# A hybrid attention block on one core: order of logits, norm pieces, sums and feed-forward products

## The chip, the cores and the metric

One core of one Trainium2 chip. The metric is device time in microseconds (us), the median of several executions. The engines are TensorE (PE, matmul; PEld is its weight load), VectorE (DVE), ScalarE (ACT), GpSimd (POOL) and SyncE (SP), which issues most DMAs here.

## What is computed

One layer over 16 learned meta tokens and 1024 frames (L = 1040, D = 1024, 8 heads of 64, feed-forward width FF = 2816), all in float32. Cut to what matters:

```python
n1 = _rmsnorm(h, norm1_w)
q, k, v, fg, u = jnp.split(n1 @ w_in, [D_ATTN, 2 * D_ATTN, 3 * D_ATTN, 3 * D_ATTN + N_HEADS], axis=-1)
# q and k are RMS-normed per head; cum_logf = cumsum(log_sigmoid(fg + b_fgate))
s = q @ k.T * scale + (cum_logf[t] - cum_logf[s])        # causal, per head
a_out = softmax(s) @ v
p_out = pooled(u) @ w_pool * pool_scale                  # trailing means minus self
h = h + jnp.concatenate([a_out, p_out], axis=-1) @ w_out
n2 = _rmsnorm(h, norm2_w)
h = h + (silu(n2 @ w_gate) * (n2 @ w_up)) @ w_down       # the meta tokens are dropped
```

## The kernel before, in words

Everything is kept transposed (features on partitions, tokens on the free axis). A float32 operand is split into a high part and a rest (fp32r), and a product is three products on TensorE: high by high, rest by high, high by rest. No scheduler reorders anything: the order in which the Python code issues instructions is the order on each engine's queue, and the tables at the top of the file (`MAXN`, `FILL`, `XN`, `XW`, `PRE`, ...) set it.

**Ramp.** Norm 1, then the projections. `v_mm` (L248) makes v for 128 tokens, 24 products of 512 columns. Behind the third block of v stand the sums of squares over the features, for the norm: 18 products of 2 columns (L281, L282; the result of a token lies on its partition) and six of a third of the tokens (L294, L295; the result lies in a row), each row evacuated by VectorE to `qrow` (L296).

**Attention.** The work is cut in 16 *units*, (head, half): units 0 to 7 are the eight heads for the first 512 query tokens, with 640 keys, units 8 to 15 the same heads for the second 512, with 1040 keys. A unit has three things:

- `stack` (L581): six loads of Q and K from DRAM and two small ones, issued by SyncE into new slots.
- `mx_steps` (L613): the logits by query rows, in chunks, for the rows' maximum: products `s`, each followed by a maximum on VectorE into `mp`. Then `mt` (L640) transposes the maximum (`Mc`) into the rows of Q that the next thing uses. In units 0 to 7 these are 5 chunks, in units 8 to 15 9 chunks.
- `sp_steps` (L658): the logits by key rows, in steps: `st` products, two exponentials on ScalarE (`ph`, `p32`), their rest `pl` on GpSimd or VectorE, and some steps later the value products `pv`, with the last of a unit followed by the division. A unit of the first half has 3 steps, one of the second half 7.

The head loop (L1188 on) goes through the units' steps. While unit n's steps run, `max_next(MAXN[n][x])` issues so many chunks of the maxima of the units ahead; `fill` issues `FILL[n]` of a product job per step of the output projection (`o` products, with loads `wos` of its weights and `h` of the residual); `work` takes one piece from a list of background pieces for SwiGLU's norm (sums of squares, `n2`, scaling, splitting of h); `vload` (L597), at step 2, issues the load of v for unit n+1 into one of two alternating slots, `vhb[h % 2]`, which the value products of unit n-1 have to have left. At the top of a unit `stack` is issued for unit n+3 (n < 6) or n+2. SyncE carries out its queue in order, so a load that waits holds up what stands behind it.

**SwiGLU.** The gate and up products of a pair of feature blocks and their weights, over both token halves, are done by a scheme with seven products for eight (`SEQ7`; `w_prep`, L1077, makes the sums and differences of the weights on VectorE and splits them; `t_pieces`, L1173, makes those of the tokens, T1 to T4). The first pair is done by all eight ordinary products (`first_pair`, L1246), first for token half 0, then, when half 1 is normed, for half 1. Between the two, `run_stream(0, 4 * PRE)` does those products of the next `PRE` pairs that need token half 0 alone (j = 1, 2). The norm of half 1 hangs on `t` (L850), which VectorE makes from the sum of squares. Then the down projection follows.

Of the kernel before, what the change touches and what calls it, by code (L numbers as in the profile page):

```python
# [8 lines left out]
FR = mybir.dt.float32r  # L9
AF = mybir.ActivationFunctionType  # L10
OP = mybir.AluOpType
AX = mybir.AxisListType

D = 1024
KT = D // 128
# [8 lines left out]
ST = 9  # L24
# [1 line left out]
BIG = 1e30  # L26
CH3 = ((0, 348), (348, 346), (694, 346))
CHQ = ((16, 512), (528, 512))
PRE = 1
VC, VK = 640, 6  # L30
SQ = 4
RA, LW = 10, 4
# [2 lines left out]
TL = 3  # L35
HL, LL, LS = 8, 5, 2
LA = 3
MAXN = [(2, 2, 1)] * 7 + [(3, 3, 3)] + [(2, 2, 1, 1, 1, 1, 1)] * 8
SUBV = 4
MID = 1  # L40
VST = 3
AGE = 2
RAMP = 1
FILL = [8 / 24] * 8 + [12 / 35] * 5 + [4 / 14] * 2 + [2 / 7]
CJ, XW, XN = {1: (0, 1), 2: (2, 3), 3: (4, 5), 4: (6, 7)}, 2, 12


@with_exitstack
def block_kernel(ctx, tc, hT, n1w, w_f, w_v, w_u, w_qk, b_f, qnw, knw, w_pool, pscale, w_out, n2w, w_g, w_up, w_d, outT):
# [12 lines left out]
    def ut(cols, dt=FT, s="u"):  # L62
        return U.tile([128, cols], dt, tag="u", bufs=NU, padded_shape=None, name=nm(s))
# [4 lines left out]
    def ps(s="ps"):  # L68
        return PSP.tile([128, 512], FT, tag="ps", name=nm(s))
# [175 lines left out]
    vst, vsd = [], DR.tile([ST, 128, 192 * NH], FT, name="vsd")  # L245
    rcol = const([128, ST], FT, "rcol")

    def v_mm(j):  # L248
        sz = min(128, L - 128 * j)
        T = slice(128 * j, 128 * j + sz)  # L250
        p = ps("v")
        for k in range(KT):
            vh, vl = wv[k // 2]
            W = slice(512 * (k % 2), 512 * (k % 2) + 512)
            mm(p[:sz], xh[k][:, T], vh[:, W], start=k == 0, stop=False)  # L255
            mm(p[:sz], xh[k][:, T], vl[:, W], start=False, stop=False)
            mm(p[:sz], xl[k][:, T], vh[:, W], start=False, stop=k == KT - 1)
        return p

    def v_evac(j, p):  # L260
# [8 lines left out]
            V.scalar_tensor_tensor(t[:sz, :, 128:192], src, rcol[:sz, j:j + 1], f(t)[:sz, :, 0:64], op0=OP.mult, op1=OP.subtract)  # L269
            nc.sync.dma_start(vsd[j, :sz, 768 * i:768 * i + 768], f(t)[:sz].rearrange("p h c -> p (h c)"))  # L270

    v0, v1, vp = v_mm(0), v_mm(1), v_mm(2)


    acch, accl = split_w(sqacc, L, ut, A, V)
    rb = ut(L, FT, "rb")
    qrow = ut(L, FT, "qrow")
    pc = ps()
    for j in range(ST):
        sz = min(128, L - 128 * j)  # L280
        mm(pc[:sz, 2 * j:2 * j + 2], acch[:, 128 * j:128 * j + sz], ones[:, 0:2], start=True, stop=False)  # L281
        mm(pc[:sz, 2 * j:2 * j + 2], accl[:, 128 * j:128 * j + sz], ones[:, 0:2], start=False, stop=True)  # L282
    qcol = const([128, ST], FT, "qcol")
    rtmp = const([128, ST], FT, "rtmp")
    V.memset(qcol, 1.0)
# [3 lines left out]
    A.activation(rcol, qcol, AF.Ln)  # L289
    A.activation(rcol, rcol, AF.Exp, scale=-0.5)  # L290
    rsqrt_newton(rcol, qcol, rtmp)
    for c, (o, n) in enumerate(CH3):
        p = ps()
        mm(p[:, :n], ones, acch[:, o:o + n], start=True, stop=False)  # L294
        mm(p[:, :n], ones, accl[:, o:o + n], start=False, stop=True)  # L295
        V.tensor_scalar(qrow[:, o:o + n], p[:, :n], 1.0 / D, EPS, op0=OP.mult, op1=OP.add)  # L296

    qkd = {c: DR.tile([NP, 2, 128, L], FT, name=f"{c}d") for c in "qk"}  # L300
# [280 lines left out]
    def stack(h, b):  # L581


        dma = nc.sync.dma_start
        T, B = slice(0, 64), slice(64, 128)
        R = (T, B)[h % 2]
        n = 640 + 400 * b
        Q, K1, K2 = ut(1024, FR, "Q"), ut(n, FR, "K1"), ut(n, FR, "K2")
        Q1, Q2 = Q[:, :512], Q[:, 512:]
        heads[h, b] = Q1, Q2, K1, K2  # L590
        q, k = [[qkd[c][h // 2, a, R, S] for a in range(2)] for c, S in (("q", slice(512 * b, 512 * b + 512)), ("k", slice(0, n)))]
        for t, P, src in ((Q1, T, q[0]), (K1, T, k[0]), (Q1, B, q[0]), (K1, B, k[1]), (Q2, T, q[1]), (K2, T, k[0])):
            dma(f(t)[P], src)
        dma(f(Q2)[64:66], f(KAT[0])[4 * h + 2:4 * h + 4, :512])
        dma(f(K2)[64:68], f(KAT[0])[4 * h:4 * h + 4, :n])

    def vload(h, b):  # L597
        for t, j, n, sz in ((0, 0, 5, 128), (1, 5, 3, 128), (1, 8, 1, 16))[:1 + 2 * b]:
            o, nj = j - 5 * t, 5 - t
            if vhb[h % 2][t] is None:  # L600
                vhb[h % 2][t] = ut(192 * nj, FR, "vh").rearrange("p (j c) -> p j c", c=192)
            nc.sync.dma_start(f(vhb[h % 2][t])[:sz, o:o + n], vsd[j:j + n, :sz, 192 * h:192 * h + 192].rearrange("j p c -> p j c"))

    bg = []
# [191 lines left out]
    for k in range(KT):  # L796
        W = slice(128 * k, 128 * k + 128)
        for p, (o, n) in zip(pb, CHQ):
            mm(p[:, :n], wcur[0][:, W], xh[k][:, o:o + n], start=k == 0, stop=False)
            mm(p[:, :n], wcur[1][:, W], xh[k][:, o:o + n], start=False, stop=False)  # L800
            mm(p[:, :n], wcur[0][:, W], xl[k][:, o:o + n], start=False, stop=k == KT - 1)
        turn()
        if k == 0:
            psplit[0] = split_w(pooled[0], SEQ, ut, A, V)
            h_load(0)
            wo[1] = out_load(1)
        if k == 1:
            h_load(1)
            stack(*units[0])
            vload(*units[0])  # L810
            stack(*units[1])
        if 2 <= k < 6:
            pool_map(5 - k)
        if k == 6:
            wo[0] = out_split(wo[0])
# [67 lines left out]
    def work(n):  # L883

        while n and (pq or dl):
            now, dl[:] = dl[:], []
            if pq:
                pq.pop(0)[1]()
            for _, g in now:
                g()  # L890
            n -= 1
# [41 lines left out]
    def finish(age):  # L933
        while fins and fins[0][2] <= step - age:
            u, g, _ = fins.pop(0)
            g()
            ready.add(u)
# [257 lines left out]
    for n, (h, b) in enumerate(units):  # L1195
        while (h, b) not in ready:
            if any(u == (h, b) for u, _, _ in fins):
                finish(0)
            else:
                max_next(1)  # L1200
        while len(heads) < min(len(units), n + (4 if n < 6 else 3)):
            stack(*units[len(heads)])
        if n == len(units) - 1:
            pq.extend((None, lambda u=u, c=c: w0_prep(u, c)) for c in (11, 21, 12, 22) for u in range(2))
            w0_load()
        for x, (front, mid, back, end) in enumerate(sp_steps(h, b)):
            step += 1
            finish(AGE)
            front()
            now, ends[:] = ends[:], []  # L1210
            mids.append(mid)
            if len(mids) > MID:
                mids.pop(0)(V if step % SUBV == 0 or n == len(units) - 1 else G)
            if n == len(units) - 1 and x:
                work(XW)
            elif n >= XN:
                work(1)
            flush()
            max_next(MAXN[n][x])
            for e in now:  # L1220
                e()
            behind.append((back, end))
            if len(behind) > LA:
                g, e = behind.pop(0)
                g()
                if e:
                    e[0]()
                    ends.append(e[1])
            background(3)
            if x == 2 and n + 1 < len(units):  # L1230
                vload(*units[n + 1])
            share += FILL[n]
            while share >= 1:
                fill(1)
                share -= 1
# [64 lines left out]
        if k >= W1:  # L1300
            w_ahead(k - KT)
    first_pair(0, second_half)
    run_stream(0, 4 * PRE)
    first_pair(1, lambda k: None)
    w0.clear()
    stores()
    run_stream(4 * PRE, len(stream))
    stores()


# [145 lines left out]
```

## Time and profile before

| | us |
|---|---|
| median of 3 executions | 1162.12 |
| the three | 1162.23, 1158.40, 1162.12 |
| the profiled execution | 1158.39 |
| its span in the profile | 1156.6 |
| mean granted clock of TensorE | 0.987 |
| TensorE busy (5327 matmuls) | 1123.7 (97%) |
| VectorE, ScalarE, GpSimd busy | 788.0 (68%), 486.1 (42%), 228.0 (20%) |
| chain that ended last: TensorE, VectorE, ScalarE, DMA | 89%, 4%, 3%, 1% |

The profile is of one execution. Its busy times tell how much of the span an engine worked; the waits tell what ended an engine's idle time; the stretches tell both for a part of the span. The granted clock is 1.00 at TensorE's full speed of 2.4 GHz and 0.50 at 1.2 GHz.

### The profile page before, as it was taken

How to read it: one execution, taken by the hardware profiler on the slowest of the kernel's cores; microseconds unless marked ns; L12 is line 12 of the kernel's file. 1: busy time of each engine (PE TensorE's matmuls, PEld its weight loads, DVE VectorE, ACT ScalarE, POOL GpSimd, SP SyncE). 2: the span in 40 equal slices, each digit the busy share in tenths (PEclk: the TensorE clock that was granted, in tenths of full speed). 3: DMA queues.
4: the chain of work that ended last, by engine and by line, in shares of the span. 5: the costliest groups of instructions: out<-in, count | busy, mean ns of one | idle time of the engine just before them, and what ended most of it. 6: DMA issues, size and time to landing. Idle time of an engine off the chain costs nothing.

```text
span 1156.6 us, 14780 instructions
## 1 busy us (share of the span) xinstructions
PE 1123.7 (97%) x5327; PEld 932.7 (81%) x5327; DVE 788.0 (68%) x1292; ACT 486.1 (42%) x883; POOL 228.0 (20%) x189
## 2 busy tenths in 40 slices
PE   7999999999999988898999999999999999999998
PEld 6778899788878876686888888888888888888886
DVE  7655874776655659747976666656665669778986
ACT  7344531535545655635433232223223335343541
POOL 0011244134336744220011001201120110000000
PEclk9999999999989998998999999999999999999999
DMA  7133340677655473050213132312231379543452
GB/s 239 75 143 134 128 151 24 180 219 186 165 145 149 111 215 115 28 164 19 100 56 109 55 100 64 110 55 92 73 100 64 113 272 370 189 157 101 153 193 110
DMA packets 72825, 151.15 MB, mean 131 GB/s; under 512 B 8752, under 2 KB 24752, under 8 KB 72752
## 3 DMA queue, kind: packets, MB, share of 16 engines
q1 hardware_dynamic: 62928, 133.91, 37.0%
q10 hardware_dynamic: 9824, 16.30, 3.9%
q8 instruction: 42, 0.69, 0.2%
q14 instruction: 31, 0.25, 0.1%
HBM read 115.13 MB, written 34.77 MB: 130 GB/s over the span
## 4 chain that ended last, share of the span: by engine, by line
PE 89%; DVE 4%; ACT 3%; DMA 1%; issue 1%; SPq 0%; POOL 0%; ACTq 0%; DVEq 0%; POOLq 0%
PE gu L1103 11%; PE gu L1104 11%; PE gu L1102 11%; PE d L1363 6%; PE d L1365 6%; PE d L1364 6%; PE pj L448 3%; PE pj L449 3%; PE pj L447 3%; PE o L502 2%; PE o L501 2%; PE o L503 2%; PE s L632 2%; PE st L684 1%; PE s L629 1%; PE v L255 1%
## 5 line engine op out<-in xcount | busy, mean ns | idle before, releaser
L1103 PE MATMUL gu<-cb,ws 128*128 128x512 f32 x560 | 220.8, 394 | 0.0
L1104 PE MATMUL gu<-cb,ws 128*128 128x512 f32 x560 | 220.7, 394 | 0.0
L1102 PE MATMUL gu<-cb,ws 128*128 128x512 f32 x560 | 220.4, 394 | 0.0
L1092 ACT ACTIVATE ws<-wst 128x512 fp32r<-128x512 f32 x120 | 70.2, 622 | 142.1 <-DVE wst L1087 96.3
L1093 DVE TENSOR_TENSOR ws<-wst,ws 128x512 fp32r<-128x512 f32 x120 | 82.5, 688 | 63.6 <-ACT ws L1092 63.6
L1103 PEld LDWEIGHTS gu<-cb,ws 128*128 128x128 f32 x560 | 105.3, 188 | 24.9 <-DVE ws L1093 0.4
L1102 PEld LDWEIGHTS gu<-cb,ws 128*128 128x128 f32 x560 | 105.3, 188 | 24.4
L1104 PEld LDWEIGHTS gu<-cb,ws 128*128 128x128 f32 x560 | 105.3, 188 | 24.1
L1363 PE MATMUL d<-hd,wd 128*128 128x512 f32 x308 | 121.1, 393 | 0.0
L1365 PE MATMUL d<-hd,wd 128*128 128x512 f32 x308 | 120.9, 393 | 0.0
L1364 PE MATMUL d<-hd,wd 128*128 128x512 f32 x308 | 120.8, 392 | 0.0
L1116 POOL TENSOR_TENSOR e<-e,e 128x512 f32<-128x512 f32 x20 | 29.1, 1457 | 333.4 <-DVE e L1129 174.1
L633 DVE TENSOR_REDUCE mp<-s 128x1 f32<-128x264 f32 (+8 forms) x112 | 54.0, 505 | 40.8 <-PE s L632 38.8
L698 POOL TENSOR_TENSOR pl<-p,ph 128x512 fp32r<-128x512 f32 (+4 forms) x58 | 69.9, 1213 | 48.0 <-ACT p L692 33.8
L448 PE MATMUL pj<-xh,wl 128*128 128x346 f32 (+2 forms) x216 | 72.9, 337 | 0.0
L449 PE MATMUL pj<-xl,wh 128*128 128x346 f32 (+2 forms) x216 | 72.9, 337 | 0.0
L447 PE MATMUL pj<-xh,wh 128*128 128x346 f32 (+2 forms) x216 | 72.9, 337 | 0.0
L691 ACT ACTIVATE ph<-st 128x512 fp32r<-128x512 f32 (+3 forms) x88 | 46.2, 525 | 54.5 <-PE st L684 52.5
L1365 PEld LDWEIGHTS d<-hd,wd 128*128 128x128 f32 x308 | 57.8, 188 | 13.2
L1364 PEld LDWEIGHTS d<-hd,wd 128*128 128x128 f32 x308 | 57.9, 188 | 13.1
L1363 PEld LDWEIGHTS d<-hd,wd 128*128 128x128 f32 x308 | 57.8, 188 | 12.9
L1032 ACT ACTIVATE hd<-wst 128x512 fp32r<-128x512 f32 x77 | 48.0, 623 | 36.0 <-issue 26.8
(279 smaller groups left out, 2421.8 us busy)
## 6 DMA issues: line engine op xcount, KB each, us to landing
wst<-in_w_d SPq DMA_DIRECT2D x77, 256.0 KB
wst<-in_w_g SPq DMA_DIRECT2D x22, 512.0 KB
wst<-in_w_up SPq DMA_DIRECT2D x22, 512.0 KB
wst<-hidd SPq DMA_DIRECT2D x22, 512.0 KB
vh<-vsd SPq DMA_DIRECT2D x16, 480.0 KB
K<-kd SPq DMA_DIRECT2D x24, 260.0 KB
vsd<-vst SPq DMA_DIRECT2D x16, 384.0 KB
Q<-qd SPq DMA_DIRECT2D x48, 128.0 KB
```

Of the source, the lines that this page charges most:

```text
L447: mm(p[:, :n], wh[:, W], xh[k][:, o:o + n], start=k == 0, stop=False)
L448: mm(p[:, :n], wl[:, W], xh[k][:, o:o + n], start=False, stop=False)
L449: mm(p[:, :n], wh[:, W], xl[k][:, o:o + n], start=False, stop=k == KT - 1)
L698: sub.tensor_tensor(pl[:sz, o0:o1], p32[:sz, o0:o1], f(ph)[:sz, o0:o1], op=OP.subtract)
L1092: A.activation(t[:, :512], src, AF.Copy)
L1093: E.tensor_tensor(t[:, 512:], src, f(t)[:, :512], op=OP.subtract)
L1102: mm(p, w[:, W], c[:, :512], start=k == 0, stop=False)
L1103: mm(p, w[:, Wl], c[:, :512], start=False, stop=False)
L1104: mm(p, w[:, W], c[:, 512:], start=False, stop=k == 3)
L1363: mm(p, w[:, W], h[:, LO], start=i == 0, stop=False)
L1364: mm(p, w[:, Wl], h[:, LO], start=False, stop=False)
L1365: mm(p, w[:, W], h[:, HI], start=False, stop=i == NPR - 1)
```

## The change

Five things are edited. `MAXN`: in the first half 2 chunks at each of the three steps of a unit, for 2, 2 and 1 (and 3, 3, 3 at unit 7). `XN`, `XW`: from unit 10 on (for unit 12) one background piece is taken at the head of each step, ahead of the `st` products, for one behind them, and the last unit takes no longer two; `FILL` spreads the output projection's jobs otherwise. `PRE`: the j = 1, 2 products of pairs 1 and 2 (for pair 1) come first in the stream, and 4 of the 8 still stand ahead of `first_pair(1)`, the other 4 behind it and ahead of the products with T's. The sums in the ramp stand one behind each product of the third block of v, with `qrow` ahead of `qcol` on VectorE. The four slots of v are allocated in the ramp, for at the first loads.

```diff
--- before.py
+++ after.py
@@ -26,7 +26,7 @@
 BIG = 1e30
 CH3 = ((0, 348), (348, 346), (694, 346))
 CHQ = ((16, 512), (528, 512))
-PRE = 1
+PRE = 2
 VC, VK = 640, 6
 SQ = 4
 RA, LW = 10, 4
@@ -35,14 +35,14 @@
 TL = 3
 HL, LL, LS = 8, 5, 2
 LA = 3
-MAXN = [(2, 2, 1)] * 7 + [(3, 3, 3)] + [(2, 2, 1, 1, 1, 1, 1)] * 8
+MAXN = [(2, 2, 2)] * 8 + [(2, 2, 1, 1, 1, 1, 1)] * 8
 SUBV = 4
 MID = 1
 VST = 3
 AGE = 2
 RAMP = 1
-FILL = [8 / 24] * 8 + [12 / 35] * 5 + [4 / 14] * 2 + [2 / 7]
-CJ, XW, XN = {1: (0, 1), 2: (2, 3), 3: (4, 5), 4: (6, 7)}, 2, 12
+FILL = [9 / 24] * 8 + [9 / 21] * 3 + [8 / 35] * 5
+CJ, XW, XN = {1: (0, 1), 2: (2, 3), 3: (4, 5), 4: (6, 7)}, 2, 10
 
 
 @with_exitstack
@@ -245,16 +245,18 @@
     vst, vsd = [], DR.tile([ST, 128, 192 * NH], FT, name="vsd")
     rcol = const([128, ST], FT, "rcol")
 
-    def v_mm(j):
+    def v_mm(j, between=()):
+        between = list(between)
         sz = min(128, L - 128 * j)
         T = slice(128 * j, 128 * j + sz)
         p = ps("v")
         for k in range(KT):
             vh, vl = wv[k // 2]
             W = slice(512 * (k % 2), 512 * (k % 2) + 512)
-            mm(p[:sz], xh[k][:, T], vh[:, W], start=k == 0, stop=False)
-            mm(p[:sz], xh[k][:, T], vl[:, W], start=False, stop=False)
-            mm(p[:sz], xl[k][:, T], vh[:, W], start=False, stop=k == KT - 1)
+            for a, (x, w) in enumerate(((xh, vh), (xh, vl), (xl, vh))):
+                mm(p[:sz], x[k][:, T], w[:, W], start=k + a == 0, stop=k + a == KT + 1)
+                if between:
+                    between.pop(0)()
         return p
 
     def v_evac(j, p):
@@ -269,17 +271,28 @@
             V.scalar_tensor_tensor(t[:sz, :, 128:192], src, rcol[:sz, j:j + 1], f(t)[:sz, :, 0:64], op0=OP.mult, op1=OP.subtract)
             nc.sync.dma_start(vsd[j, :sz, 768 * i:768 * i + 768], f(t)[:sz].rearrange("p h c -> p (h c)"))
 
-    v0, v1, vp = v_mm(0), v_mm(1), v_mm(2)
+    v0, v1 = v_mm(0), v_mm(1)
 
 
     acch, accl = split_w(sqacc, L, ut, A, V)
     rb = ut(L, FT, "rb")
     qrow = ut(L, FT, "qrow")
     pc = ps()
-    for j in range(ST):
+
+    def col(j, a):
         sz = min(128, L - 128 * j)
-        mm(pc[:sz, 2 * j:2 * j + 2], acch[:, 128 * j:128 * j + sz], ones[:, 0:2], start=True, stop=False)
-        mm(pc[:sz, 2 * j:2 * j + 2], accl[:, 128 * j:128 * j + sz], ones[:, 0:2], start=False, stop=True)
+        mm(pc[:sz, 2 * j:2 * j + 2], (acch, accl)[a][:, 128 * j:128 * j + sz], ones[:, 0:2], start=a == 0, stop=a == 1)
+
+    def row(o, n):
+        p = ps()
+        mm(p[:, :n], ones, acch[:, o:o + n], start=True, stop=False)
+        mm(p[:, :n], ones, accl[:, o:o + n], start=False, stop=True)
+        V.tensor_scalar(qrow[:, o:o + n], p[:, :n], 1.0 / D, EPS, op0=OP.mult, op1=OP.add)
+
+    sums_of = [lambda j=j, a=a: col(j, a) for j in range(ST) for a in range(2)]
+    for x, (o, n) in zip((18, 12, 6), CH3):
+        sums_of.insert(x, lambda o=o, n=n: row(o, n))
+    vp = v_mm(2, sums_of)
     qcol = const([128, ST], FT, "qcol")
     rtmp = const([128, ST], FT, "rtmp")
     V.memset(qcol, 1.0)
@@ -289,12 +302,6 @@
     A.activation(rcol, qcol, AF.Ln)
     A.activation(rcol, rcol, AF.Exp, scale=-0.5)
     rsqrt_newton(rcol, qcol, rtmp)
-    for c, (o, n) in enumerate(CH3):
-        p = ps()
-        mm(p[:, :n], ones, acch[:, o:o + n], start=True, stop=False)
-        mm(p[:, :n], ones, accl[:, o:o + n], start=False, stop=True)
-        V.tensor_scalar(qrow[:, o:o + n], p[:, :n], 1.0 / D, EPS, op0=OP.mult, op1=OP.add)
-
 
 
     qkd = {c: DR.tile([NP, 2, 128, L], FT, name=f"{c}d") for c in "qk"}
@@ -596,9 +603,7 @@
 
     def vload(h, b):
         for t, j, n, sz in ((0, 0, 5, 128), (1, 5, 3, 128), (1, 8, 1, 16))[:1 + 2 * b]:
-            o, nj = j - 5 * t, 5 - t
-            if vhb[h % 2][t] is None:
-                vhb[h % 2][t] = ut(192 * nj, FR, "vh").rearrange("p (j c) -> p j c", c=192)
+            o = j - 5 * t
             nc.sync.dma_start(f(vhb[h % 2][t])[:sz, o:o + n], vsd[j:j + n, :sz, 192 * h:192 * h + 192].rearrange("j p c -> p j c"))
 
     bg = []
@@ -807,6 +812,8 @@
         if k == 1:
             h_load(1)
             stack(*units[0])
+            for a in range(4):
+                vhb[a % 2][a // 2] = ut(192 * (5 - a // 2), FR, "vh").rearrange("p (j c) -> p j c", c=192)
             vload(*units[0])
             stack(*units[1])
         if 2 <= k < 6:
@@ -1206,15 +1213,13 @@
         for x, (front, mid, back, end) in enumerate(sp_steps(h, b)):
             step += 1
             finish(AGE)
+            if n >= XN:
+                work(1)
             front()
             now, ends[:] = ends[:], []
             mids.append(mid)
             if len(mids) > MID:
                 mids.pop(0)(V if step % SUBV == 0 or n == len(units) - 1 else G)
-            if n == len(units) - 1 and x:
-                work(XW)
-            elif n >= XN:
-                work(1)
             flush()
             max_next(MAXN[n][x])
             for e in now:
@@ -1300,11 +1305,11 @@
         if k >= W1:
             w_ahead(k - KT)
     first_pair(0, second_half)
-    run_stream(0, 4 * PRE)
+    run_stream(0, 4)
     first_pair(1, lambda k: None)
     w0.clear()
     stores()
-    run_stream(4 * PRE, len(stream))
+    run_stream(4, len(stream))
     stores()
```

How this moves instructions, at three places. The number behind a name tells buffers apart; in brackets stand the semaphores that an instruction waits for, where it has any.

**TensorE, unit 9's first logits.** Before, the last value product of unit 5 (`pv_578_3145`) is followed by the `st` of unit 7 and the logits `s` of unit 8:

```order
L713 MATMUL pv_578_3145<-pl_573_3126,vh_426_2490 128x144
L711 MATMUL pv_578_3145<-ph_566_3086,vh_426_2490 128x16
L712 MATMUL pv_578_3145<-ph_566_3086,vh_426_2490 64x16
L713 MATMUL pv_578_3145<-pl_573_3126,vh_426_2490 128x16
L681 MATMUL st_597_3237<-Q_513_2867,K1_514_2868 128x512 [waits PE_49,Activation_49]
L683 MATMUL st_597_3237<-maskA_79,ident_69 128x112
L684 MATMUL st_597_3237<-Q_513_2867,K2_515_2869 128x512 [waits Activation_49]
L629 MATMUL s_601_3247<-K1_541_2989,Q_540_2988 128x392 [waits DVE_49]
L631 MATMUL s_601_3247<-maskB_86,ident_69 128x128
L632 MATMUL s_601_3247<-K2_542_2990,Q_540_2988 128x392
```

and unit 9's first logits, on `K1_595_3227`, stand 48 products further on:

```order
L684 MATMUL st_617_3320<-Q_513_2867,K2_515_2869 128x144
L681 MATMUL st_617_3320<-Q_513_2867,K1_514_2868 128x16
L683 MATMUL st_617_3320<-maskA_79,ident_69 128x16
L684 MATMUL st_617_3320<-Q_513_2867,K2_515_2869 128x16
L629 MATMUL s_622_3338<-K1_595_3227,Q_594_3226 128x328 [waits DMAHW2_49,DMAHW1_49,DMAHW3_49,DMAHW0_49,DVE_49]
L632 MATMUL s_622_3338<-K2_596_3228,Q_594_3226 128x328 [waits DMAHW6_49,DMAHW7_49,DMAHW5_49,DMAHW4_49]
```

In the order of the change unit 5's last value product is the first four rows here, and unit 9's K is `K1_607_3279` and `K2_608_3280`:

```order
L718 MATMUL pv_589_3196<-pl_585_3181,vh_336_2021 128x144
L716 MATMUL pv_589_3196<-ph_577_3136,vh_336_2021 128x16
L717 MATMUL pv_589_3196<-ph_577_3136,vh_336_2021 64x16
L718 MATMUL pv_589_3196<-pl_585_3181,vh_336_2021 128x16
L686 MATMUL st_609_3289<-Q_522_2907,K1_523_2908 128x512 [waits PE_49,Activation_49]
L688 MATMUL st_609_3289<-maskA_79,ident_69 128x112
L689 MATMUL st_609_3289<-Q_522_2907,K2_524_2909 128x512
L634 MATMUL s_614_3301<-K1_607_3279,Q_606_3278 128x328 [waits DMAHW3_49,DMAHW2_49,DMAHW4_49,DMAHW1_49,DVE_49]
L637 MATMUL s_614_3301<-K2_608_3280,Q_606_3278 128x328 [waits DMAHW6_49,DMAHW7_49,DMAHW5_49,DMAHW0_49]
```

Three products now stand between the two, for 48.

**SyncE, the loads of Q and K of unit 9.** Before (v's slot of the odd heads is `vh_426_2490`):

```order
L602 DMA vh_335_2020<-vsd_356 128x5x192 [waits DMAHW6_49,PE_49]
L602 DMA vh_426_2490<-vsd_356 128x5x192 [waits DMAHW7_49,PE_49]
L593 DMA Q_594_3226<-qd_480 64x512 [waits DMAHW0_49,Activation_49]
L593 DMA K1_595_3227<-kd_481 64x1040 [waits DMAHW1_49]
L593 DMA Q_594_3226<-qd_480 64x512 [waits DMAHW2_49]
L593 DMA K1_595_3227<-kd_481 64x1040 [waits DMAHW3_49]
L593 DMA Q_594_3226<-qd_480 64x512 [waits DMAHW4_49]
L593 DMA K2_596_3228<-kd_481 64x1040 [waits DMAHW5_49,Activation_49,Pool_49]
```

and in the order of the change, where it is `vh_336_2021`:

```order
L607 DMA vh_335_2020<-vsd_356 128x5x192 [waits DMAHW6_49,PE_49]
L520 DMA wos_596_3221<-in_w_out 128x512 [waits PE_49,DMAHW7_49,Activation_49,Pool_49]
L607 DMA vh_336_2021<-vsd_356 128x5x192 [waits DMAHW0_49,PE_49]
L600 DMA Q_606_3278<-qd_480 64x512 [waits DMAHW1_49]
L600 DMA K1_607_3279<-kd_481 64x1040 [waits DMAHW2_49]
L600 DMA Q_606_3278<-qd_480 64x512 [waits DMAHW3_49]
L600 DMA K1_607_3279<-kd_481 64x1040 [waits DMAHW4_49]
L600 DMA Q_606_3278<-qd_480 64x512 [waits DMAHW5_49]
L600 DMA K2_608_3280<-kd_481 64x1040 [waits DMAHW6_49]
```

In both, v's load for unit 7, which waits for TensorE, stands right ahead of them; a slice of the output weights, `wos`, has moved ahead of that load.

**VectorE, ahead of the norm of the second token half.** Before:

```order
L1116 TENSOR_TENSOR eg_1107_5364<-gu_1066_5113,eg_1107_5364 128x512
L1085 TENSOR_TENSOR s1_1108_5368<-wst_1091_5260 128x512
L1086 TENSOR_TENSOR wst_1091_5260<-wst_1090_5258,wst_1091_5260 128x512
L1087 TENSOR_TENSOR wst_1090_5258<-s1_1108_5368,wst_1090_5258 128x512
L1093 TENSOR_TENSOR ws_1109_5372<-wst_1090_5258,ws_1109_5372 128x512
L850 TENSOR_SCALAR t2_1113_5393<-n2_1112_5392 128x512
L1093 TENSOR_TENSOR ws_1115_5400<-wst_1091_5260,ws_1115_5400 128x512
L146 TENSOR_TENSOR tm2_1118_5418<-t2_1113_5393,r2_1114_5397 128x512
```

and in the order of the change:

```order
L1123 TENSOR_TENSOR eg_1111_5372<-gu_1066_5113,eg_1111_5372 128x512
L1100 TENSOR_TENSOR ws_1112_5376<-wst_1094_5266,ws_1112_5376 128x512
L857 TENSOR_SCALAR t2_1116_5397<-n2_1115_5396 128x512
L1100 TENSOR_TENSOR ws_1118_5404<-wst_1096_5270,ws_1118_5404 128x512
L146 TENSOR_TENSOR tm2_1121_5422<-t2_1116_5397,r2_1117_5401 128x512
L147 SCALAR_TENSOR_TENSOR tm2_1121_5422<-tm2_1121_5422,r2_1117_5401 128x512
```

The three weight sums of L1085 to L1087 stood ahead of `t2` (L850, L857 in the change) and no longer do.

## Rows read from the trace of the kernel before

**Rows 1.** The page, busy time of each engine over the whole span.

```profile
PE 1123.7 (97%) x5327; PEld 932.7 (81%) x5327; DVE 788.0 (68%) x1292; ACT 486.1 (42%) x883; POOL 228.0 (20%) x189
```

**Rows 2.** TensorE's waits by line: waited for, us in total, times, longest.

```profile
PE pv L713 <- POOL pl L698: 3.7, 2, 2.1
PE pv L713 <- DVE pl L698: 3.4, 2, 2.0
PE gu L1259 <- ACT cb L869: 2.4, 1, 2.4
PE gu L1261 <- DVE cb L870: 2.2, 1, 2.2
...
PE s L632 <- DMA K<-kd: 1.5, 1, 1.5
PE ps L294 <- DVE qrow L296: 0.9, 1, 0.9
```

**Rows 3.** Stretches: us; busy by engine (instructions); granted clock, DMA share, GB/s.

```profile
44.89:49.05 4.16, 3.27 (x25) 2.63 (x24) 1.58 (x7) 1.94 (x7) 0.00 (x0) 1.00 0.00 0
...
323.64:333.88 10.24, 9.45 (x33) 7.87 (x32) 4.68 (x8) 2.78 (x5) 1.45 (x2) 0.50 0.66 167
...
410.00:450.00 40.00, 34.87 (x195) 29.03 (x194) 29.90 (x53) 26.22 (x54) 20.79 (x18) 1.00 0.49 146
450.00:486.00 36.00, 28.42 (x122) 21.73 (x123) 31.27 (x45) 21.89 (x48) 11.94 (x10) 0.86 0.28 93
480.65:484.06 3.41, 2.90 (x7) 2.35 (x8) 2.66 (x5) 0.42 (x1) 1.25 (x1) 0.50 0.36 111
532.10:542.10 10.00, 5.42 (x14) 3.53 (x13) 8.68 (x14) 5.72 (x9) 0.00 (x0) 0.66 0.00 0
```

**Rows 4.** Chain of waits, 312 to 324: start us, us, what.

```profile
312.57 0.12 PE pv L713
...
316.34 6.62 DMA K<-kd
...
323.05 0.39 PE s L632
```

**Rows 5.** SyncE's issues, 312 to 317: start us, us, line, what.

```profile
312.71 0.38 SPq L602 DMA_DIRECT2D vh<-vsd  x1
...
316.34 0.53 SPq L593 DMA_DIRECT2D K<-kd  x1
```

**Rows 6.** Stretch from that value product to unit 9's first logits.

```profile
312.54:321.19 8.65, 8.65 (x51) 7.72 (x50) 6.39 (x13) 4.24 (x8) 3.67 (x4) 1.00 0.88 204
```

**Rows 7.** TensorE's instructions, two of the 18 small sums.

```profile
45.03 0.25 PE L281 MATMUL ps<-ones,wh 128*128 128x2 f32 x1
45.14 0.25 PE L282 MATMUL ps<-ones,wl 128*128 128x2 f32 x1
```

**Rows 8.** VectorE's instructions ahead of the norm of token half 1.

```profile
522.02 0.68 DVE L1085 TENSOR_TENSOR s<-wst 128x512 f32<-128x512 f32 x1
...
525.46 0.69 DVE L850 TENSOR_SCALAR t<-n 128x512 f32<-128x512 f32 x1
```

**Rows 9.** Stretches with products of the kinds that the new order puts there.

```profile
312.54:313.20 0.66, 0.66 (x5) 0.57 (x5) 0.00 (x0) 0.48 (x1) 0.66 (x1) 1.00 0.00 0
348.85:351.90 3.05, 3.05 (x16) 2.62 (x15) 1.80 (x3) 1.87 (x4) 1.47 (x2) 1.00 0.82 188
303.47:308.71 5.24, 5.24 (x28) 4.42 (x28) 3.92 (x10) 2.31 (x4) 2.08 (x3) 1.00 0.70 224
303.47:311.23 7.76, 7.76 (x50) 6.83 (x49) 5.51 (x13) 3.79 (x7) 3.12 (x4) 1.00 0.48 153
351.90:361.46 9.56, 9.56 (x54) 8.20 (x53) 4.90 (x11) 6.78 (x13) 5.82 (x6) 1.00 0.40 112
```

**Rows 10.** SyncE's issues at 413: the spills of h.

```profile
413.82 5.13 SPq L833 DMA_DIRECT2D h2d<-h  x8
```

## The prediction

> **What bounds the kernel now.** I read the summary of the page first: TensorE is busy for 1123.7 us of a span of 1156.6 [rows 1], so a change of order can win only what TensorE waits, plus what it works at its lower clock. The list of TensorE's waits says where they are [rows 2], and the table of stretches what each costs [rows 3]: under 1 us in the ramp at 45 us, a stall at 321 to 334, the second half of attention (410 to 486), and the start of the SwiGLU's second norm (532 to 542). That is nearly all there is to win. Then comes the other side, what stands ready only just in time. For this the chain of waits through 312 to 323 us [rows 4] and SyncE's row of issues there [rows 5] are the key: the last value product of a unit ends at 312.69, SyncE, whose next instruction was a load of v that waits for it, goes on at 312.71, issues the eight loads of Q and K that stand behind it, and the last half of K lands at 322.96. TensorE had wanted it 1.47 us earlier.
>
> So a unit's K lands 10.3 us after the value product that frees SyncE, and TensorE had 8.65 us of work between the two [rows 6]. I call that work the cover. The question for this change is what it makes of each unit's cover.
>
> **Part 1, what the order wins.**
>
> *Ramp.* The 24 small products and their gap take 4.16 us, of which TensorE is busy 3.27 [rows 3]. Put between v's products, they no longer wait for the evacuation of one another's banks (0.9 us [rows 2]): −0.9. Bounds: 0, if the waits only move, and −1.8, if half of the 18 tiny ones' pitch of 0.11 us (45.03 to 45.14 in [rows 7]) goes too. The earlier slots of v cost nothing: their allocation issues no instruction.
>
> *The stall at 321 to 334.* 1.47 us of wait and 10.24 us at half clock with 9.45 busy, which at full clock would be 4.7 [rows 2, 3]: −6.2 in all. The new place of this wait is priced whole in part 2, so this one goes.
>
> *410 to 486.* TensorE stands still for 5.13 + 7.58 = 12.7 us, and the mean clock of 0.86 in the second stretch means some 10 us at half clock, or 5 lost [rows 3]. VectorE is the cause: busy 31.27 of 36 us, and most of the waits end on its pl or on GpSimd's [rows 2]. Two steps of the change help: one logit chunk of each later unit is worked off earlier in the first half (6 per unit for 5), and the norm's pieces start at unit 10 for unit 12, where VectorE has room (6.39 of 8.65 us [rows 6]). I take −12.7 and leave the lost clock, because a new wait of part 2 falls into this stretch. Bounds −5, the second stretch's wait less a third, and −17.7.
>
> *532 to 542.* 4.6 us idle [rows 3]. VectorE runs three weight sums (L1085 to L1087, from 522.02 on) ahead of the t on which the norm hangs [rows 8]; the order of the change has no sums there. The first wait (2.4) should go, the second (2.2), at the end of the same chain, stay: −2.4, bounds 0 and −6.9 (both waits, and 2.3 of the 6.8 us that a mean clock of 0.66 leaves at half speed).
>
> The first-half products of a second pair ahead of the T's: no wait of TensorE for a T is among the rows, and the products are the same ones: 0, covered by the 1123.7 us of TensorE; if the cover went, one product group would wait some 2 us as at 532.
>
> Sum of part 1: −22.2 (bounds −11 and −32.6).
>
> **Part 2, what the order loses.** In the order of the change a step's background work stands elsewhere, but v's load still stands on SyncE right ahead of the next stack of Q and K. The logits now come sooner: 6 chunks per unit for 5 put them 7 chunks ahead at the end of unit 6, more than a unit of 5; unit 7 gives 6 for 9, so 4 chunks of the lead stay from then on. TensorE's cover falls by what they passed. I counted the products between the gate and the first logit product of each unit in the new order and priced them by like stretches of before [rows 6, 9].
>
> - *Unit 9.* Between the last value product of unit 5 and the first logit product of unit 9 stand three products of 512, 112 and 512 columns, as at 312.54 to 313.20: 0.66 us. Wait 10.25 − 0.66 = 9.6.
> - *Unit 10.* At most the 3.05 us of 348.85 to 351.90: 10.25 − 3.05 = 7.2; up to 8.2 if all three loads of v (two more issues of 0.4 to 0.5 us [rows 5]) stand ahead.
> - *Unit 8.* 28 products as at 303.47 to 308.71: 5.24. Bare wait 5.0; with a slice of the output weights and a row of h (256 and 512 KB) ahead of it on the queue, which at the 204 GB/s of [rows 6] take 3.8 us, 8.8. I take 7.
> - *Unit 6.* 50 products, 7.76 us. It loads only 640 columns, so I scale the landing (my estimate: 3.63 us of issue and 640/1040 of 6.62 make 7.7): no wait when bare, 3.7 with the same 768 KB ahead. I take 3.
> - *Units 5 and 7.* Cover 6 us or more against 7.7: 1 together, bounds 0 and 3.4.
> - *Unit 14.* The eight spills of h now stand between v's load and this stack; they take 5.13 us of issue [rows 10]. Cover some 54 products, 9.56 us: 10.25 + 5.13 − 9.56 = 5.8; before, SyncE's pause for v's load hid part of it, so I take 5, bounds 0 and 5.9.
>
> Units 11, 12, 13 and 15 keep over 10 us: 0. Sum 32.8, bounds 21.8 (bare loads, nothing for units 5, 6, 7 and 14) and 39.6.
>
> What stands behind a wait of TensorE: all other engines, which live from its products. VectorE, GpSimd and ScalarE catch up meanwhile; that is in part 1.
>
> *The clock.* The wait of 1.47 us at 321 us was followed, from 323.64 on, by 10.24 us at a granted clock of 0.50, which is 1.2 of 2.4 GHz [rows 3]; the waits in 410 to 450 us, 5.1 us in sum, left it at 1.00. For waits of 5 to 10 us before has no row. Four such waits (units 8, 9, 10, 14) at some 6.8 us of half clock each cost 4 x 3.4 = 13.6; bounds 4 x 1.7 (half of a spell of 3.4 as at 480.65 [rows 3]) and 4 x 5.1 (half of 10.24).
>
> The Trainium skill ("TensorE: Matmul & The Clock Gate", section "HAM oscillation — how this bites in real kernels") says that a TensorE which works in bursts with waits for DMA between them starts every burst throttled again. The trace half agrees: the one DMA wait here was followed by the lower clock, the waits for VectorE mostly not. By the page the sum would be that of rival C below, without it the sum that now follows.
>
> **Sum.** −22.2 + 32.8 + 13.6 = +24.2 on the profiled execution of 1158.4: 1182.6. That execution was the fastest of three; the median is 1162.1, 3.7 above. I put the changed kernel's median at **1185**.
>
> **The rivals.**
>
> *A, the waits feed the rest (faster).* Mechanism: at a long wait for K, VectorE, GpSimd and ScalarE empty their queues, so every later wait for them goes, and the loads, alone on the queues, land at the low bound. For it: the waits after 410 us all are for those engines [rows 2]. Price: −32.6 and 21.8 − 6 for units 8 and 10 landing sooner, without lower clock: 1158.4 − 16.8 = 1141.6, about 1145 as a median. It decides once the K waits with their clock cost less than some 26 us. Against it: 9.6 + 7.2 us for units 9 and 10 alone rest on a landing time that the trace shows, and must be beaten by waits that sum to 33 us in the whole kernel. Chance 0.07.
>
> *B, it balances.* Waits at 21.8, lower clock at 6.8, gains between the sum's and their best, −27: +1.6, median 1160 to 1168. Chance 0.12.
>
> *C, every wait is paid for by the long spell of lower clock.* Six waits x 5.1 = 30.7 for 13.6: 1158.4 − 22.2 + 32.8 + 30.7 = 1199.7, about 1203. For it: the one DMA wait of before did so. Against it: units 8, 9 and 10 follow each other closely, so spells overlap. Chance 0.12.
>
> *D, VectorE's waits stay* (the norm's pieces only move the crowd from 440 to 480 to the stretch before it), gains at −11: 1158.4 − 11.2 + 46.4 = 1193.6, about 1197. Chance 0.12.
>
> *E, the K waits don't arise*, because the loads are released by something earlier than I read from the order: then −22.2 alone, 1136 to 1140. Against it: SyncE's row shows the issue 0.02 us after the value product [rows 4, 5]. Chance 0.03.
>
> Forecast as it stands: 0.54.
>
> **Numbers.** A measurement of this kernel can tell about 0.5%, or 5.8 us, from no change. A and E are faster (0.10); of B two thirds lie within 0.5% (0.08); the rest of B, the forecast, C and D are slower (0.82). Range: from the middle of B, 1159, to the upper part of C, 1206; outside it lie A, E, and what C and D have beyond, some 0.17. Faster and slower both are in the cases, but the forecast's own range, 1173 to 1197, holds most of the chance.
>
> **What would show it.** Right: the list of TensorE's waits headed by the logit products, waiting for DMA of K, 20 us and more in four to six waits of 3 to 10 us at 280 to 350 us, the longest at unit 9 right behind three products of st; on SyncE v's load ending with the last value product; the mean clock under 1.00 in the slices behind; waits of pv, mt and o after 410 us down by half or more; the t at 525 us without three sums ahead; no wait at 48 us. Wrong: K waits under 15 us in sum, or the first of each unit's loads issued well before the value product; or the waits after 410 us as before, which would put the time near D.

## The result and the profile after

The changed kernel takes 1203.68 us (median; 1203.64 to 1205.55) against 1160.26 for the kernel before on the same chip: ratio 1.0388, 95% interval 1.0344 to 1.0432. It is 43 us slower; the profiled executions, 1203.64 and 1158.39, differ by 45.2. The forecast, 1185 in a range up to 1206, had the sign, the place and the mechanism of the loss, and about half its size (24.2 of 45.2 us on the profiled executions).

The page's busy times after, over the whole span of 1201.8 us, answer to [rows 1]:

```profile
PE 1141.5 (95%) x5327; PEld 944.5 (79%) x5327; DVE 793.6 (66%) x1292; ACT 486.0 (40%) x883; POOL 230.5 (19%) x189
```

TensorE executes as many products as before and is busy 17.8 us longer; more of them run at the lower clock (below). The other 27.4 of the 45.2 us are idle time (60.3 for 32.9). TensorE's waits after (waited for, us in total, times, longest) answer to [rows 2]:

```profile
PE s L634 <- DMA K<-kd: 24.2, 6, 7.2
PE s L637 <- DMA K<-kat: 7.7, 6, 1.8
...
PE mt L657 <- DVE Mc L652: 3.7, 1, 3.7
PE mt L657 <- DVE mp L622: 3.7, 1, 3.7
PE pv L718 <- DVE pl L703: 2.5, 3, 1.4
PE gu L1266 <- DVE cb L877: 2.4, 1, 2.4
PE gu L1264 <- ACT cb L876: 1.2, 1, 1.2
PE v L257 <- DVE vst L271: 1.1, 1, 1.1
```

Waits for K, of which there were 1.5 us, now head the list: 24.2 + 7.7 and half a microsecond more, 32.4 us. The waits for VectorE that the change was to remove are still there, at other lines. TensorE's instructions at unit 9 show the longest:

```profile
330.55 0.26 PE L718 MATMUL pv<-pl,vh 128*128 128x16 f32 x1
330.66 0.47 PE L686 MATMUL st<-Q,K 128*128 128x512 f32 x1
330.97 0.21 PE L688 MATMUL st<-maskA,ident 128*128 128x112 f32 x1
331.02 0.46 PE L689 MATMUL st<-Q,K 68*128 68x512 f32 x1
338.71 0.61 PE L634 MATMUL s<-K,Q 128*128 128x328 f32 x1 [7.22 <-DMA K<-kd]
340.47 0.64 PE L637 MATMUL s<-K,Q 66*128 66x328 f32 x1 [1.16 <-DMA K<-kat]
```

and SyncE's issues there, the load of v and the two ends of the stack behind it, with the last step of the chain of waits:

```profile
330.84 0.38 SPq L607 DMA_DIRECT2D vh<-vsd  x1
331.26 0.54 SPq L600 DMA_DIRECT2D Q<-qd  x1
...
335.72 0.64 SPq L602 DMA_DIRECT2D K<-kat  x1
```

```profile
335.72 4.71 DMA K<-kat
340.43 0.04 issue
340.47 0.64 PE s L637
```

The last value product of unit 5 ends, v's load goes out at 330.84, the stack follows, and K's last rows land at 340.43, 9.6 us later. In between stand the three products of the order, 0.7 us of work. This is [rows 4, 5] with the cover of [rows 6] taken away.

The granted clock behind each of these waits (stretches: us, busy by engine, clock, DMA share, GB/s):

```profile
289.28:292.69 3.41, 3.41 (x9) 2.64 (x8) 0.00 (x0) 0.89 (x2) 0.00 (x0) 0.50 0.70 206
309.76:316.59 6.83, 4.28 (x12) 3.58 (x13) 1.00 (x2) 0.48 (x2) 3.24 (x3) 0.50 0.29 62
333.66:343.90 10.24, 4.04 (x14) 3.16 (x15) 2.35 (x4) 0.00 (x0) 0.00 (x0) 0.50 0.54 127
357.55:371.20 13.65, 9.80 (x34) 8.42 (x35) 3.76 (x7) 3.87 (x7) 1.28 (x1) 0.50 0.43 108
429.23:432.64 3.41, 3.41 (x10) 2.63 (x9) 0.51 (x1) 0.00 (x0) 0.00 (x0) 0.50 0.00 0
449.71:459.95 10.24, 9.21 (x32) 8.00 (x33) 3.41 (x6) 3.87 (x7) 1.27 (x1) 0.50 0.39 103
```

The six spells add up to 47.8 us at 1.2 GHz, with TensorE busy 34.2 of them. At 2.4 GHz that work would have taken about half as long, so I estimate the cost of these spells at 17 us. Before there was one such spell behind a wait for K, with 9.45 busy [rows 3].

The end of the second half of attention, behind the last wait for K, and the second norm; by content these answer to the last stretches of [rows 3]:

```profile
460.00:530.00 70.00, 59.55 (x278) 47.14 (x277) 56.03 (x83) 42.01 (x92) 29.86 (x23) 0.88 0.28 83
575.00:585.00 10.00, 6.41 (x19) 4.53 (x18) 9.38 (x16) 5.89 (x9) 0.45 (x1) 0.72 0.00 0
```

TensorE still stands still for 10.5 us in the first, where VectorE is busy 56 of 70 us, and for 3.6 in the second, where it was 4.6.

### The profile page after: what moved, and what is told of

It is laid out like the page before. It is cut to its first block, busy times and chain, and to the rows that moved or that the text cites. A ratio compares the mean times of both kernels' runs of the same rounds, so it can differ in the third digit from the quotient of the medians.

```text
span 1201.8 us, 14770 instructions
## 1 busy us (share of the span) xinstructions
PE 1141.5 (95%) x5327; PEld 944.5 (79%) x5327; DVE 793.6 (66%) x1292; ACT 486.0 (40%) x883; POOL 230.5 (19%) x189
## 4 chain that ended last, share of the span: by engine, by line
PE 85%; DVE 4%; DMA 4%; ACT 3%; SPq 2%; issue 1%; POOL 1%; ACTq 0%; POOLq 0%; DVEq 0%
PE gu L1110 10%; PE gu L1111 10%; PE gu L1109 10%; PE d L1370 6%; PE d L1368 6%; PE d L1369 6%; PE v L257 4%; PE pj L455 3%; PE pj L456 3%; PE pj L454 3%; DMA K<-kat 2%; PE o L508 2%; PE o L509 2%; PE o L510 2%; PE s L637 1%
```

## The experiments

The theory at this point (K): the new `MAXN` lets the logits of units 6 to 10, 13 and 14 overtake their K, whose loads stand on SyncE behind a load of v that waits for TensorE. The rival (V): the norm's pieces, and VectorE with them, make the loss.

**The new MAXN alone**, in the kernel before:

```diff
-MAXN = [(2, 2, 1)] * 7 + [(3, 3, 3)] + [(2, 2, 1, 1, 1, 1, 1)] * 8
+MAXN = [(2, 2, 2)] * 8 + [(2, 2, 1, 1, 1, 1, 1)] * 8
```

> Kernel before with the new MAXN alone. Theory K (the logits of units 5 to 10 overtake the loads of K, which stand on SyncE behind a load of v that waits for TensorE): this edit alone makes waits of s for K at units 6 to 10 of some 25 us in sum and spells of lower clock behind them, so 1190 to 1205 us, nearly all of the loss of the whole change. Rival V (the norm's pieces at the head of the steps, with VectorE behind, make the loss from 410 us on): the logits matter little, 1155 to 1170 us.

Measured: 1188.8 us, ratio 1.0278 (1.0256 to 1.0299). K's waits in its list:

```profile
PE s L629 <- DMA K<-kd: 13.7, 4, 7.8
...
PE s L632 <- DMA K<-kd: 3.7, 3, 1.5
PE s L632 <- DMA K<-kat: 3.4, 3, 1.7
```

20.8 us, somewhat less than expected, and the time is just under the expected range. One table of numbers, alone, costs 31.6 us; rival V is out as the main cause.

**The old MAXN back**, in the changed kernel (the same diff reversed).

> The changed kernel with the old MAXN, all else kept. Theory K: the K waits of units 5 to 10 are gone or below 3 us in sum, the waits after 410 us stay much as in the changed kernel: 1160 to 1172 us. Rival V: the loss stays for the larger part, 1180 us or more.

Measured: 1150.41 us, ratio 0.9945 (0.993 to 0.996). The only wait for K left is this one:

```profile
PE s L637 <- DMA K<-kat: 1.6, 2, 0.9
```

The rest of the change is worth having: 6.8 us faster than before. My own expectation was 10 us too high, since it took the waits after 410 us to be as in the changed kernel; in attention they fell from 18.6 to 6.8 us, and 8.2 of the 18.6 were K's, at units 13 and 14. Within the change `MAXN` costs 1203.7 − 1150.4 = 53 us (51 by the ratios), against 31.6 alone: the waits for K are 32.4 us for 20.8, and of those after 410 us the run with `MAXN` alone has 0.8. Which of the other edits makes the table dearer was not tested.

**v's load behind the stack**, in the changed kernel. This leaves the order of every product and gives K's loads an earlier gate:

```diff
             stack(*units[len(heads)])
+        if n:
+            vload(*units[n])
...
-            if x == 2 and n + 1 < len(units):
-                vload(*units[n + 1])
```

> The changed kernel with v's load of a unit moved from step 2 of the unit before to the top of its own unit, behind the stack of Q and K that is issued there; all else kept. Theory K: the gate of each stack is now a unit earlier (some 9 us more cover), so the 32 us of waits for K fall below 5 and most of the lower clock in 280 to 400 us with them: 1145 to 1165 us. Rival V: VectorE's work was done during the waits for K, and comes back as waits for mp, Mc and pl of 20 us and more: 1175 to 1195 us.

Measured: 1164.01 us, ratio 1.0063 (1.0048 to 1.0078). K's waits are 7.5 us, not below 5, but 39.7 us have come back.

```profile
PE s L637 <- DMA K<-kat: 3.3, 2, 1.9
PE s L634 <- DMA K<-kd: 2.8, 3, 1.2
...
PE s L637 <- DMA K<-kd: 1.4, 1, 1.4
```

With this the cause is shown from its other side: nothing of TensorE's order was touched, only what stands ahead of K on SyncE.

**The same in the kernel before.**

> The kernel before with the same move of v's load. Theory K: the wait of 1.5 us for unit 9's K and the 10.24 us of half clock behind it go, 5 to 6 us faster than before, and v lands in time (no wait of pv for v). Rival: something else is late at 321 us (Q's row of maxima from ScalarE, 0.8 us), the clock falls all the same, and nothing is measured: within 2 us of before.

Measured: 1156.26 us, ratio 0.9984 (0.9971 to 0.9996). The wait for K and the spell of lower clock behind it are gone from the trace, but the gain is 0.9 us (1.9 by the ratio), not 5. The time is the rival's, but not for its reason, since the clock does not fall there any more. In the profile waits of another kind have come, none of them large:

```profile
PE mt L652 <- DVE Mc L647: 3.4, 3, 2.2
...
PE st L684 <- ACT Q L653: 1.2, 1, 1.2
...
PE pv L711 <- DMA vh<-vsd: 0.7, 1, 0.7
```

Before, mt's waits were 2.1 us and st's for Q 0.8; the last is v, which now comes late. TensorE's idle time is 32.7 us for 33.0, so the 1.5 us taken away came back nearly whole, the largest rise at mt; one profile each doesn't settle how much of the missing 4 us that is.

**v's load behind the stack and the stack always four units ahead**, in the changed kernel (`n + (4 if n < 6 else 3)` becomes `n + 4`).

> The changed kernel with v's load behind the stack and the stack always issued four units ahead (before: three from unit 6 on). Theory K: the last 7.5 us of waits for K in the run with v behind the stack alone come from the units whose stack is issued three ahead; they go, and 1150 to 1158 us are left, the rest being VectorE's waits for Mc and mp, which the new MAXN makes. Rival: the waits for K move to the slots (SyncE waits for a slot of K instead), 1162 us or more.

Measured: 1159.37 us, ratio 1.0001 (0.9986 to 1.0015). The time is 1.4 us above the expected range. Waits for K are down to 1.4 us, and 44.3 of the 53 us are back. What is left, 8.5 us over the best order of this page (1150.85), is hardly due to K; the waits for mt are 6.5 us, 1.2 in the best order:

```profile
PE mt L657 <- DVE Mc L652: 6.5, 2, 3.3
...
PE s L637 <- DMA K<-kd: 1.4, 1, 1.4
```

**The transposes of the maxima one step later** (`AGE = 3` for 2), on top of the last.

> The run with v behind the stack and the stack four ahead, and in addition the maxima's transposes mt three steps behind the unit's last chunk of logits for two (AGE 3). Without waits for K the new MAXN still cost 9 us against the old one; theory M: that is mt, which TensorE reaches while VectorE still makes Mc (6.5 us of waits and the lower clock behind them); one step later Mc is made, and 1150 to 1155 us are left. Rival: VectorE is full there, and the wait moves to the next of its products (mp, pl): 1157 us or more.

Measured: 1155.35 us, ratio 0.9975 (0.996 to 0.9989), between the two theories. mt's waits fall from 6.5 to 4.2 us, in two rows:

```profile
PE mt L657 <- DVE Mc L652: 3.4, 2, 1.9
...
PE mt L657 <- DVE mp L622: 0.8, 1, 0.8
```

The time falls by 4.0 us (3 by the ratios, whose intervals just touch). Waits have come elsewhere (`st` for VectorE's results, 2.2 us for none; `pv` for `pl`, 4.5 us for 3.4, GpSimd's among them), and TensorE's idle time in the two profiled executions doesn't fall: 32.1 us for 31.5. So mt has a part in the 8.5 us, but how large it is isn't shown; that waits move on to VectorE's other results is as the rival said.

**The norm's pieces and FILL alone**, in the kernel before:

```diff
-FILL = [8 / 24] * 8 + [12 / 35] * 5 + [4 / 14] * 2 + [2 / 7]
+FILL = [9 / 24] * 8 + [9 / 21] * 3 + [8 / 35] * 5
...
             finish(AGE)
+            if n >= XN:
+                work(1)
             front()
...
-            if n == len(units) - 1 and x:
-                work(XW)
-            elif n >= XN:
-                work(1)
```

with `XN` 10 for 12.

> Kernel before with the norm's pieces from unit 10 on at the head of each step, the last unit's second pieces left out, and the new FILL; the old MAXN, PRE, ramp and slots. With the old MAXN back in the whole change the time was 1150.4 us, 6.8 below before. Theory N: most of that is this part, whose pieces start two units sooner than VectorE's full stretch at 440 to 480 us: 1150 to 1154 us, the waits after 410 us down from 12.7 us to 9 or less. Rival: this part moves VectorE's full stretch only, and the gain is from the earlier slots of v, which set K's loads free sooner: 1156 to 1162 us.

Measured: 1153.4 us, ratio 0.9951 (0.9932 to 0.9969), as much as the whole change without `MAXN`. The two stretches of [rows 3] read in it:

```profile
410.00:450.00 40.00, 34.90 (x184) 28.68 (x184) 35.87 (x58) 26.36 (x55) 19.95 (x15) 0.96 0.42 99
450.00:486.00 36.00, 32.89 (x159) 26.13 (x159) 25.89 (x43) 22.20 (x49) 13.05 (x12) 0.95 0.29 95
```

VectorE's full stretch has moved forward (35.87 of the first 40 us busy, before 29.90; 25.89 of the next 36, before 31.27), and TensorE stands still for 8.2 us in both together instead of 12.7. Not all of the 6 us need come from there: the spell of 10.24 us behind unit 9's wait is missing too, though TensorE waits for K at 325 and 338 us, 0.6 and 1.0 us long.

**Two pairs' products ahead, alone** (`PRE = 2`, the first stream still of four).

> Kernel before with the first-half products of two pairs ahead (PRE 2), all else kept. Theory K: the three weight sums no longer stand ahead of the norm's t, the first wait of gu for ScalarE's cb falls from 2.4 to about 1.2 us, the second stays at 2.4; 1 to 3 us faster than before. Rival: the products only move, and the wait moves with them to the T's or to the weights: within 1 us.

Measured: 1157.87 us, ratio 0.9994 (0.9979 to 1.0009). The first wait falls and the second stays, both as expected, and the time can't tell 1 us:

```profile
PE gu L1261 <- DVE cb L870: 2.4, 1, 2.4
...
PE gu L1259 <- ACT cb L869: 1.2, 1, 1.2
```

**The ramp alone** (the small sums one per product, v's slots taken early).

> Kernel before with the ramp's part alone: the small sums one behind each product of the third block of v, and v's slots allocated in the ramp. The trace of the change showed the wait for qrow (0.9 us) gone and a wait for vst (1.1 us) in its place. Theory: nothing is won here, within 2 us of before, the same exchange of the two waits. Rival: the earlier slots of v set K's loads free sooner, and a gain of 3 us or more shows at 280 to 340 us.

Measured: 1158.57 us, ratio 0.9992 (0.9975 to 1.0009): no difference. The wait of 0.9 us for `qrow` is gone, and in its place stands

```profile
PE v L257 <- DVE vst L271: 1.1, 1, 1.1
```

**The best order: old MAXN, rest of the change, v's load behind the stack.**

> The changed kernel with the old MAXN and v's load behind the stack. Theory K: with the old MAXN only 1.6 us of waits for K are left, so the move of v's load has 0 to 2 us to win: 1148 to 1151 us. Rival: with SyncE free sooner K and Q of later units take the slots and the DMA engines from v and the weights, new waits for v: 1153 us or more.

Measured: 1150.85 us, ratio 0.9927 (0.9904 to 0.9949). Not to be told apart from the run without the move; both beat the kernel before.

**The same with the transposes one step later.**

> The best order so far (the change with the old MAXN and v's load behind the stack) and in addition mt three steps behind for two. Theory M: the waits of mt there are 1.2 us, so 0 to 3 us are to be won: 1147 to 1151 us. Rival: Q's rows of maxima come later and st waits for them (1.2 us now): 1153 us or more.

Measured: 1158.18 us, ratio 1.0 (0.9984 to 1.0015). A miss: the rival held. What helps the one order hurts the other, for `st` of eight units now waits for the rows that mt writes:

```profile
PE st L689 <- ACT Q L658: 6.4, 8, 1.2
```

## Why the prediction was right in kind and half in size

**Where the missing half lies.** The forecast's sum was +24.2 us on the profiled execution, the measured one +45.2: 21.0 us are missing. The forecast has waits for K of 31.3 us more than before, and 30.9 were measured. It has 16.0 us less of all other waits (0.9 + 12.7 + 2.4), and 3.5 were measured: 12.5 us of the miss. It has 8.9 us for the lower clock (13.6 behind the new waits, less 4.7 for the old one), and TensorE's busy time grew by 17.8: 8.9 us of the miss. That the time still came 2 us under the top of the range is in part luck: the top was set by rival C alone, and what happened is D's outcome with more of the lower clock than the forecast has, which no case put together.

**The waits for K: right, unit by unit.** The forecast's sum was 32.8 us, the measured one 32.4; that the sums agree so closely is luck, since the units of the forecast make 29.0 and one that it left out the rest. From TensorE's instructions after, with the forecast in brackets: unit 6 2.0 (3), unit 7 0.9 (1, with unit 5, which has none), unit 8 5.6 (7), unit 9 8.4 (9.6), unit 10 7.3 (7.2), unit 14 4.9 (5), and unit 13 3.3, which the forecast gave none. Unit 13 was missed because I counted only v's load as a gate; ahead of its stack 10.32 us go by over two loads of the output weights, the second of which waits 9.5 us for a GpSimd instruction (`sq`, L565) to end:

```profile
402.44 6.69 SPq L607 DMA_DIRECT2D vh<-vsd  x3
409.23 10.32 SPq L520 DMA_DIRECT2D wos<-in_w_out  x2
419.61 0.51 SPq L600 DMA_DIRECT2D Q<-qd  x1
```

The last row is the start of unit 13's stack; K was wanted from 424.4 on and came at 425.85. In the run with v's load behind the stack such loads still stand ahead of that stack, and its wait is still 2.9 us:

```profile
374.96 15.67 SPq L520 DMA_DIRECT2D wos<-in_w_out  x3
```

That the waits are K's gate, and not something else in the new order, is shown by the two runs that move the gate: 32.4 us fall to 7.5 and 1.4.

**The lower clock: too low.** The step was "Four such waits ... at some 6.8 us of half clock each cost 4 x 3.4 = 13.6". The runs showed six spells of 3.4 to 13.65 us, 47.8 in all for 27 forecast. Behind the seven waits for K only the shortest, unit 7's 0.9 us, brought no fall. Rival C, with six spells of 10.24, 61 us, erred on the other side; the measured 47.8 lie between it and the forecast. In cost they are nearer to the forecast, some 17 us for its 13.6 and C's 30.7, since TensorE was busy only 34.2 of the 47.8 us. By the rule of the Trainium skill that stands in the prediction ("TensorE: Matmul & The Clock Gate", "HAM oscillation — how this bites in real kernels"), every such burst starts slow: the trace agrees for six of seven waits. The rest of the miss in the clock lies elsewhere: there are four spells in the rest of attention and SwiGLU, 23.9 us in sum, for 17.1 in three before. Together with those behind K the spells from 280 us on to the last products are 71.7 us for 27.3; half of the 44.4 more would be 22, and TensorE's busy time says 17.8, since it waited through a part of them.

**The gain of 12.7 us in 410 to 486: failed inside this change.** The step counted on VectorE having room from unit 10 on (the row that it gives, [rows 6], is from unit 7) and on the chunks worked off earlier as a help. The first half of that is right: alone, the norm's pieces give 6 us (1153.4), as waits of 12.7 fall to 8.2 and spells of 10.2 us in that place to 6.8. The second half is wrong: with hardly a wait for K the new chunks still cost 8.5 us, and waits for mt of 1.2 us in the best order are 6.5. So the two about cancel, and the change keeps 10.3 of the 12.7 us in waits of mt and pv, 7.4 of them at mt, which TensorE reaches before VectorE has made Mc. The prediction had named this as a sign of being wrong, the waits after 410 us as before, near D. It is rival D's outcome, but not its reason, since alone the pieces win. Why VectorE is later with Mc under the new table stays open.

**Ramp and second norm: small, and smaller than said.** −0.9 became 0, since v's next block then waits until VectorE has evacuated an earlier one (vst); −2.4 became −1.0 (4.6 to 3.6 us of waits), as only the wait for ScalarE's cb hung on the three sums.

**Rival A fell.** Little comes back later as waits saved: TensorE's idle time grew by 27.4 us and the waits for K by 30.9, so all others fell by 3.5. **E fell** with the first row of the list of waits.

What stays open: how much of the 4 us that v's load behind the stack should have given the kernel before went to VectorE's waits, and why spells of the clock behind like waits are 3.4 us once and 13.65 another time.

## What to carry to other kernels

Where an order brings work forward, count for each of its operands how much work is left between the event that frees the load and the first use, and set that against the time from issue to landing in the trace: here it gave the waits to about 1.5 us each before anything was run, but for the one whose gate was overlooked: every wait in the issuing queue counts, not only the one that shows in the trace of before. Count the lower clock behind such waits as well; it cost more than half as much as the waits themselves. A load that waits for the consumer should not stand ahead of loads that are wanted sooner: moving it gave 40 of 53 us back without touching a product. Where TensorE had enough other work in between, as in the kernel before, the same move gave 1 to 2 us.

## What was not expected of the hardware

VectorE's two instructions on 4 columns that make Mc take 0.17 us each or, at times, several times that. The trace after gives for one of them (minimum, median, maximum in ns)

```profile
L651 DVE TENSOR_SCALAR Mc<-mx x16: 171/204/1274, 246.0 to 496.6; 128x4 fp32r<-128x4 f32 x16
```

and all that take over 0.2 us, of this one and of the next (L652), lie beside an instruction of GpSimd with two inputs and end within 0.04 us of such an instruction's end; in the run with the stack four ahead, VectorE's and GpSimd's instructions at one of the waits of mt are these:

```profile
425.51 0.17 DVE L650 TENSOR_REDUCE mx<-mp 128x4 f32<-128x12 f32 x1
425.71 1.24 DVE L651 TENSOR_SCALAR Mc<-mx 128x4 fp32r<-128x4 f32 x1
426.98 1.18 DVE L652 SCALAR_TENSOR_TENSOR Mc<-mx,Mc 128x4 fp32r<-128x4 f32 x1
```

```profile
425.65 2.48 POOL L703 TENSOR_TENSOR pl<-p,ph 128x512 fp32r<-128x512 f32 x2
```

2.1 of the 3.3 us that mt waits there are this. The Trainium skill ("GPSIMD Engine Reference", section "1. Specifications") states that the two engines share their interfaces to SBUF, and contend where VectorE runs in one of its 2-port modes or reads two inputs from SBUF. The trace agrees for L652, which reads two (mx and Mc), with 1.18 us for an instruction of 0.17; L651 reads one and takes up to 1.27 us, and no row tells its mode. No run here took GpSimd's work away, so that it is the cause is argued from where the two lie, not shown.
